# Turning the second token half without GpSimd: g_ffn inside ScalarE's copies, T1 from B11's digits, operands in kept weight rooms

## The chip, the cores and the metric

The kernel runs on one core of a Trainium2 chip. The metric is the device time of one execution in microseconds, and the time given for a kernel is the median of its runs.

## What is computed

One encoder layer for 1024 tokens of width 1024 in fp32. The part that matters here is its end:

```
x  = x + merged @ w_out                  # output projection, residual
h2 = rmsnorm(x, g_ffn)                   # x * rsqrt(mean(x^2) + eps) * g_ffn
x  = x + square(relu(h2 @ w_up)) @ w_down    # 1024 -> 4096 -> 1024
```

Before it stand a first norm, a combined projection, a pooling mixer and a differential attention with eight heads, whose two branches are gated and merged.

## The kernel before

**Digits.** The matrix engine TensorE works on fp32r operands. Each fp32 operand is split into a high digit (a ScalarE copy that rounds, line 125) and a low digit (the difference, line 126, on VectorE or GpSimd). `mm3` (lines 131 to 133) multiplies two such operands in three matmuls: hi x hi, hi x lo, lo x hi.

**Seven products.** Each large product is cut into 2 x 2 blocks and made of seven block products instead of eight (Strassen's scheme in Winograd's form). The right operand of the up projection is h2 transposed, with four blocks: B11 and B21 (the upper and lower 512 features of the first 512 tokens) and B12 and B22 (those of the second 512). From them come T1 = B12 - B11, T2 = B22 - T1, T3 = B22 - B12 and T4 = (B21 - B11) - T3. The left operand is w_up, taken in 16 pairs of 128-column blocks (`up_pair`). The first half of a pair multiplies A11 and A12 with B11 and B21 (banks X and Y, "1" and "2"); its second half makes the sums S1 to S4 of the weight blocks and multiplies them with T2, T1, T3, T4 and B22 ("6", "5", "7", "4", "3"). The first halves of four pairs (AHEAD = 4) need only B11 and B21.

**The output projection's tail.** The string `O_TAIL` writes the order out by hand: "7t" and "4t" are the last products for token tile t (128 tokens) of the second half, "nt" turns tile t of the first half. A product's bank is added to its partial sum by VectorE (L791), and the result is stored to `yd` (L950).

**Norm and turn.** `norm_scale` squares a token tile on ScalarE (L964), forms the mean on VectorE (L965, L256) and its power -1/2 on GpSimd (L257), scales the rows by it on ScalarE (L968) and multiplies by g_ffn, broadcast over the partitions as `gfb`, on VectorE (L971). `norm_turn` transposes eight 128x128 blocks on TensorE (L980) into two PSUM banks `hb`. For the first token half, `first_half` splits the banks into digits of B11 and B21, and stores a copy r11 of the turned B11 and d21 = B21 - r11 to DRAM (`nd`, L993, L994). For the second half, `second_half` loads r11 back into t1 (L1097), has VectorE subtract it from the bank (L1099: T1) and the result from the other bank (L1100: T2), and has ScalarE copy both banks over the tile y (L1102, L1103). `combine` then makes the digits of T1, T3, B22 and T4; the subtractions for T3 and T4 (L1113, L1119) and T3's low digits run on GpSimd.

**Rooms.** Left operands of the up projection (`a_op`) stand in eight rooms of 4 KB per partition: two for A11 (`pw1`), six for all others (`pw`). They lie where the weight rooms of the mixing phase (pool `wpool`, tag W, eight rooms) lay, and a room waits for the last reader of the room below it. Weights of the output projection stand in those W rooms, except sets 6 and 7, which have rooms of their own (tag fw). Scratch tiles come from `ev` (nine rooms), and `finish` takes a new one for each result.

**Order.** The Tile framework orders the instructions of each engine by priorities (`tc.cur_priority`) and resources. Each engine works through its own queue in order. In the code below, `second_scale` for all four tiles and `second_half(4)` have the priorities of the steps "4t"; tiles 5 to 7 follow between the first halves of pairs 0 and 1.

Of the kernel before, what the change touches and what calls it, by code (L numbers as in the profile page):

```python
# [56 lines left out]
O_TAIL = "a0 70 n0 71 n1 72 n2 40 n3 73 41 42 43"  # L57
# [6 lines left out]
def encoder_kernel(  # L64
# [55 lines left out]
    def f(ap):  # L120
        return ap.bitcast(F32)
# [6 lines left out]
    def mm3(ps, lhs_hi, lhs_lo, rhs_hi, rhs_lo, first, last, more=False):  # L128

        kw = {"skip_group_check": True} if more else {}  # L130
        nc.tensor.matmul(ps, lhs_hi, rhs_hi, start=first, stop=False, **kw)  # L131
        nc.tensor.matmul(ps, lhs_hi, rhs_lo, start=False, stop=False, **kw)  # L132
        nc.tensor.matmul(ps, lhs_lo, rhs_hi, start=False, stop=last, **kw)  # L133
# [3 lines left out]
    def wt(shape, name, dt=F32R):  # L137

        wcount[0] += 1
        if wcount[0] > N_QKVW and (wcount[0] - N_QKVW - 1) % (N_W + N_FW) >= N_W:  # L140
            return fw_tile(shape, name, dt)
        return wpool.tile(shape, dt, tag="W", name=name, bufs=N_W)

    def fw_tile(shape, name, dt=F32R):
        return wpool.tile(shape, dt, tag="fw", name=name, bufs=N_FW)
# [255 lines left out]
    with ExitStack() as ph:  # L401
# [75 lines left out]
        nc.sync.dma_start(rows[20:21, :], g_sub)  # L477

# [441 lines left out]
    def w_room(shape, name):  # L920
        return wpool.tile(shape, F32R, tag="W", name=name, bufs=N_W)

# [35 lines left out]
    def norm_scale(t, src, sq):  # L958

        ss = const.tile([P, 2], F32, tag="nss", name=f"nss{t}", bufs=2)  # L960
        rs = const.tile([P, 1], F32, tag="nrs", name=f"nrs{t}", bufs=2)
        yn = y[t]
        for j in range(2):
            nc.scalar.activation(sq, src[j], AF.Square, accum_out=ss[:, j : j + 1])  # L964
        nc.vector.tensor_scalar(rs, ss[:, 0:1], ss[:, 1:2], 1.0 / D, op0=ALU.add, op1=ALU.mult)  # L965
        rsq(rs, rs, 1, 1.0)
        for j in range(2):
            scaled[t] = nc.scalar.activation(yn[:, j * 512 : (j + 1) * 512], src[j], AF.Copy, scale=rs)  # L968
        for j in range(2):
            js = slice(j * 512, (j + 1) * 512)  # L970
            nc.vector.tensor_tensor(yn[:, js], yn[:, js], gfb[:, js], op=ALU.mult)  # L971
# [11 lines left out]
    nd = dram.tile([2, 4, P, 4, P], F32, name="nd")  # L983

    def first_half(t):
# [7 lines left out]
        nc.sync.dma_start(nd[0, t], r11)  # L993
        nc.sync.dma_start(nd[1, t], d21)  # L994
# [6 lines left out]
    prio = {}  # L1001
# [45 lines left out]
    for step in O_TAIL.split():  # L1047
# [7 lines left out]
        elif step[0] == "a":  # L1055
            for d in range(4):
                a_set("4", d)
        elif step[0] == "n":
            first_half(t)
        else:  # L1060
            o_product(Y[t], "4", t, ws["4"])
            k = half(t, 0)
            add(dve, k, Y[t], k)
            y_done(k, 4 + t, 0)
            prio[4 + t] = tc.cur_priority
# [5 lines left out]
    pw1 = pool_of(hs, "pw1", 2)  # L1071
    pw = pool_of(hs, "pw", N_OP - 2)
# [13 lines left out]
    kept_b = {}  # L1086
    T1s, T2_made = {}, {}

    def second_scale(t):
        y[t] = py[t % 4].tile([P, D], F32, tag="y", name=f"y{t}")  # L1090
        norm_scale(t, [half(t - 4, 0), half(t, 0)], y[t][:, 0:512])

    def second_half(t):
# [8 lines left out]
        nc.scalar.copy(kept_b[t][:, 0], b12)  # L1102
        nc.scalar.copy(kept_b[t][:, 1], b22)  # L1103
        T2_made[t] = b_split("T2", c0, t2, dve)

    def combine(q):
        for t in range(4, NT):
# [26 lines left out]

    def u_product(ps, j, a):
        hi, lo = Bq[SIDES[j][1]]
        for k in range(4):
            mm3(
# [4 lines left out]
    def a_op(p, name, src, eng):  # L1143
        a = (pw1 if name == "11" else pw).tile([P, 2, 4, P], F32R, tag="op", name=f"A{name}_{p}")
# [3 lines left out]
    def up_pair(p):  # L1148
# [16 lines left out]
        def finish(q, ps, part):  # L1165
            r = ev(f"u{q}_{p}")
            add(dve, r, ps, part)
# [101 lines left out]
    hs.close()  # L1269
    mlp_ps.close()  # L1270
# [171 lines left out]
```

## Time and profile before

| | us |
|---|---|
| median of 3 runs | 1551.07 (1550.24 to 1551.65) |
| the profiled execution | 1551.25 |
| its span, first to last instruction | 1549.4 |
| granted TensorE clock, mean | 0.999 |

The span is the time from the first to the last instruction in the trace; the time of the execution has some 2 us around it. Engines are named as in the profile: PE is TensorE's matmuls, PEld its weight loads, DVE VectorE, ACT ScalarE, POOL GpSimd, SP the engine whose queue issues most DMAs. A line such as `[1.66 <-ACT y L1102]` says that the engine had been idle for 1.66 us, and that ScalarE's instruction of line 1102 on a tile y ended last of what it waited for. A trailing number in a tile's name is left out.

### The profile page before, as it was taken

What the parts mean: (1) busy time and instruction counts of PE and PEld (TensorE: products, weight loads), DVE (VectorE), ACT (ScalarE), POOL (GpSimd) and SP (SyncE); (2) the same over time, 40 slices, a digit from 0 to 9 for tenths busy, and PEclk for the clock granted to TensorE, in tenths of its full rate; (3) what the DMA queues carried; (4) which work ended last, traced back from release to release, by engine and by line L of the source; (5) the groups of instructions that cost most, each with busy time, mean ns of one, the idle gap of its engine ahead of it and who ended that gap; (6) DMA issues with size and microseconds to landing.
All of it is one profiled execution on the core that took longest, in us unless ns stands there. A gap on an engine that the chain in (4) does not pass through costs nothing. (4 is left out here: it accounts for less than half of the span.)

```text
span 1549.4 us, 21730 instructions
## 1 busy us (share of the span) xinstructions
PE 1524.4 (98%) x7601; PEld 1314.4 (85%) x7601; DVE 1025.6 (66%) x2113; ACT 801.7 (52%) x1642; POOL 411.0 (27%) x481
## 2 busy tenths in 40 slices
PE   7999999999999999999999998999999999999999
PEld 6999999999999999888888886788888788888887
DVE  7777767677777778634644898766665668556572
ACT  5656555556555655534642586555555634333331
POOL 5424242434344443219745514000000000000000
PEclk9999999999999999999999999999999999999999
DMA  7112121111112121249757434554342789537650
GB/s 226 44 53 67 37 66 44 61 51 47 58 40 68 35 88 49 73 150 377 260 170 225 148 143 143 177 177 150 136 137 109 278 314 386 175 123 258 224 190 28
DMA packets 170280, 216.37 MB, mean 140 GB/s; under 512 B 10341, under 2 KB 104250, under 8 KB 170170
## 3 DMA queue, kind: packets, MB, share of 16 engines
q1 hardware_dynamic: 152762, 187.67, 36.8%
q10 hardware_dynamic: 17408, 27.30, 4.7%
q8 instruction: 60, 0.98, 0.3%
q14 instruction: 50, 0.41, 0.1%
HBM read 156.18 MB, written 58.75 MB: 139 GB/s over the span
## 5 line engine op out<-in xcount | busy, mean ns | idle before, releaser
L131 PE MATMUL z<-wqkv,hT 128*128 128x384 f32 x512 | 175.1, 342 | 0.0
L133 PE MATMUL z<-wqkv,hT 128*128 128x384 f32 x512 | 174.2, 341 | 0.5 <-DVE hT L126 0.3
L132 PE MATMUL z<-wqkv,hT 128*128 128x384 f32 x512 | 174.4, 341 | 0.0
L627 ACT ACTIVATE s<-s,nm 128x256 f32<-128x256 f32 (+7 forms) x128 | 99.7, 780 | 74.6 <-DVE nm L619 71.7
L257 POOL TENSOR_TENSOR ms<-ms,mhalf 128x4 f32<-128x4 f32 x64 | 65.2, 1018 | 206.7 <-DVE ms L256 196.4
L131 PE MATMUL g<-hT,fwgate 128*128 128x512 f32 x256 | 101.0, 395 | 0.0
L133 PE MATMUL g<-hT,fwgate 128*128 128x512 f32 x256 | 100.6, 394 | 0.0
L132 PE MATMUL g<-hT,fwgate 128*128 128x512 f32 x256 | 100.5, 393 | 0.0
L131 PEld LDWEIGHTS z<-wqkv,hT 128*128 128x128 f32 x512 | 97.1, 190 | 2.9 <-ACT hT L125 0.6
L133 PEld LDWEIGHTS z<-wqkv,hT 128*128 128x128 f32 x512 | 96.9, 189 | 2.6 <-DVE hT L126 1.4
L132 PEld LDWEIGHTS z<-wqkv,hT 128*128 128x128 f32 x512 | 97.1, 190 | 1.7
L619 DVE CUSTOM_DVE_ANT_0 s<-sc,dist 128x512 f32<-128x512 f32 (+3 forms) x128 | 74.3, 585 | 24.2 <-PE sc L617 23.3
L126 DVE TENSOR_TENSOR AS<-s,AS 128x512 fp32r<-128x512 f32 x64 | 44.9, 705 | 34.4 <-ACT AS L125 34.4
L616 PE MATMUL sc<-K,Q 128*128 128x512 f32 (+2 forms) x192 | 67.3, 356 | 0.4 <-DVE nm L619 0.4
L126 POOL TENSOR_TENSOR wqkv<-rqkv,wqkv 128x384 fp32r<-128x384 f32 x60 | 62.9, 1062 | 14.1 <-ACT wqkv L125 11.7
L617 PE MATMUL sc<-K,Q 128*128 128x512 f32 (+2 forms) x192 | 66.1, 349 | 0.0
L126 POOL TENSOR_TENSOR fwgate<-frgate,fwgate 128x512 fp32r<-128x512 f32 x32 | 43.9, 1374 | 63.2 <-ACT fwgate L125 63.2
L133 PEld LDWEIGHTS g<-hT,fwgate 128*128 128x128 f32 x256 | 48.1, 188 | 9.6
L131 PEld LDWEIGHTS g<-hT,fwgate 128*128 128x128 f32 x256 | 48.1, 188 | 9.1 <-ACT go L375 0.2
L132 PEld LDWEIGHTS g<-hT,fwgate 128*128 128x128 f32 x256 | 48.1, 188 | 8.8
L133 PE MATMUL ba<-yT,wba 128*128 128x512 f32 x128 | 50.4, 395 | 0.0
L132 PE MATMUL ba<-yT,wba 128*128 128x512 f32 x128 | 50.4, 395 | 0.0
(452 smaller groups left out, 4625.9 us busy)
## 6 DMA issues: line engine op xcount, KB each, us to landing
wd<-in_w_down_dram SPq DMA_DIRECT2D x56, 512.0 KB, 5.6
wu<-in_w_up_dram SPq DMA_DIRECT2D x32, 512.0 KB, 5.1
udS<-us SPq DMA_DIRECT2D x64, 256.0 KB, 2.3
ur<-udS SPq DMA_DIRECT2D x32, 512.0 KB, 3.4
rqkv<-in_w_in_dram SPq DMA_DIRECT2D x64, 192.0 KB, 2.9
ud<-u ACTq DMA_DIRECT2D x48, 256.0 KB, 2.1
ur<-ud SPq DMA_DIRECT2D x24, 512.0 KB, 5.0
frgate<-in_w_gate_dram SPq DMA_DIRECT2D x32, 256.0 KB, 2.8
```

The lines of the kernel that those rows point to most:

```text
L126: return (lo_eng or nc.vector).tensor_tensor(lo, src, f(hi), op=ALU.subtract)
L131: nc.tensor.matmul(ps, lhs_hi, rhs_hi, start=first, stop=False, **kw)
L132: nc.tensor.matmul(ps, lhs_hi, rhs_lo, start=False, stop=False, **kw)
L133: nc.tensor.matmul(ps, lhs_lo, rhs_hi, start=False, stop=last, **kw)
L257: nc.gpsimd.tensor_tensor(dst, dst, mhalf[:, :n], op=ALU.pow)
L616: nc.tensor.matmul(dst, Q[:, i, 0, :], rhs, start=True, stop=False)
L617: nc.tensor.matmul(dst, Q[:, i, 1, :], rhs, start=False, stop=True)
L619: nc.vector.tensor_tensor_reduce(out=s[i][:, c : c + w], in0=sc[:, 0:w], in1=dist[:, o0 + c : o0 + c + w], scale=2.0 ** -(h + 1), scalar=B ...
L627: nc.scalar.activation(s[i][:, 0:n], s[i][:, 0:n], AF.Exp, bias=last, scale=-1.0, accum_out=Z[:, i, t : t + 1])
```

## The change

- The scaling and the turning of the second token half move into the tail's written order ("st" and "tt"): tiles 4 and 5 are turned there, into the projection's banks. Tiles 6 and 7 are turned behind product 1 of pair 0 and of pair 1 (`issue_after(made["1"])`).
- For the second half g_ffn is no longer multiplied in by VectorE before the turn. After it, features lie on the partitions, and ScalarE's copies out of the banks, now eight of 128x128 in place of two of 128x512, scale by a column of `cols`, into which g_ffn's rows are loaded at the start.
- For the first half, scaling and g_ffn become one `scalar_tensor_tensor` on VectorE.
- T1 is the kept copy less B11's high digit less its low digit; r11 is no longer stored or loaded.
- The subtractions and low digits for T3 and T4 go from GpSimd to VectorE.
- The weight rooms split into two tags of four, W0 and W1, in a pool that stays open through the up projection. Operands A11 and A12 take W0, all others W1. Of the output projection's sets, 2 and 3 take W0, and 1, 5 and 4 take W1.
- `finish` writes its sum over the partial product's scratch tile.

The power on GpSimd (L257) stays. The diff, cut to its core:

```diff
-O_TAIL = "a0 70 n0 71 n1 72 n2 40 n3 73 41 42 43"
+O_TAIL = "a0 70 n0 71 n1 72 n2 40 s0 n3 73 41 s1 42 t0 s2 43 t1 s3"
...
+    ops = ctx.enter_context(ExitStack())
+    wpool = ops.enter_context(tc.tile_pool(name="wpool", bufs=1))
...
-    wpool = mix.enter_context(tc.tile_pool(name="wpool", bufs=1))
+    fwpool = mix.enter_context(tc.tile_pool(name="fwpool", bufs=N_FW))
...
-        return wpool.tile(shape, dt, tag="W", name=name, bufs=N_W)
+        return w_tile(shape, name, (wcount[0] - 1 - (N_QKVW if wcount[0] > N_QKVW else 0)) % (N_W if wcount[0] <= N_QKVW else N_W + N_FW) // 4 % 2, dt)
+
+    def w_tile(shape, name, i, dt=F32R):
+        return wpool.tile(shape, dt, tag=f"W{int(i)}", name=name, bufs=N_W // 2)
...
+        nc.sync.dma_start(rows[21:29, :], g_ffn[0].rearrange("(r p) -> r p", p=P))
...
-        room = fw_tile if j in "67" else w_room
+        room = fw_tile if j in "67" else lambda shape, name: w_tile(shape, name, j not in "23")
...
         for j in range(2):
-            scaled[t] = nc.scalar.activation(yn[:, j * 512 : (j + 1) * 512], src[j], AF.Copy, scale=rs)
-        for j in range(2):
             js = slice(j * 512, (j + 1) * 512)
-            nc.vector.tensor_tensor(yn[:, js], yn[:, js], gfb[:, js], op=ALU.mult)
+            if t < 4:
+                nc.vector.scalar_tensor_tensor(yn[:, js], src[j], rs, gfb[:, js], op0=ALU.mult, op1=ALU.mult)
+            else:
+                scaled[t] = nc.scalar.activation(yn[:, js], src[j], AF.Copy, scale=rs)
...
-        nc.sync.dma_start(nd[0, t], r11)
-        nc.sync.dma_start(nd[1, t], d21)
+        nc.sync.dma_start(nd[t], d21)
...
+    def second_turn(t, b):
+        kept_b[t] = y[t].rearrange("p (q a b) -> p q a b", q=2, a=4)
+        for j in range(2):
+            for i in range(4):
+                k = 4 * j + i
+                nc.scalar.activation(
+                    kept_b[t][:, j, i, :], b[j][:, i, :], AF.Copy, scale=cols[:, 21 + k : 22 + k]
+                )
...
+        elif step[0] == "s":
+            second_scale(4 + t)
+        elif step[0] == "t":
+            second_turn(4 + t, norm_turn(4 + t, lambda j, name: o_bank(name, 2 * (t % 2) + j)))
...
-    pw1 = pool_of(hs, "pw1", 2)
-    pw = pool_of(hs, "pw", N_OP - 2)
...
+        if after is not None:
+            with tc.issue_after(after.ins):
+                second_turn(t, norm_turn(t, lambda j, name: bm.tile([P, 512], F32, tag="ZW"[j], name=name)))
...
-        nc.sync.dma_start(t1, nd[0, t - 4])
-        b12, b22 = norm_turn(t, lambda j, name: bm.tile([P, 512], F32, tag="ZW"[j], name=name))
-        sub(dve, t1, b12, t1)
-        sub(dve, t2, b22, t1)
-        kept_b[t] = y[t].rearrange("p (q a b) -> p q a b", q=2, a=4)
-        nc.scalar.copy(kept_b[t][:, 0], b12)
-        nc.scalar.copy(kept_b[t][:, 1], b22)
+        cs = slice(c0, c0 + P)
+        sub(dve, t1, kept_b[t][:, 0], f(Bq["11"][0][:, :, cs]))
+        sub(dve, t1, t1, f(Bq["11"][1][:, :, cs]))
+        sub(dve, t2, kept_b[t][:, 1], t1)
...
-                sub(pool, t3, b22, t3)
-                b_split(q, c0, t3, pool)
+                sub(dve, t3, b22, t3)
+                b_split(q, c0, t3, dve)
...
-                nc.sync.dma_start(b22, nd[1, t - 4])
-                sub(pool, b22, b22, t3)
+                nc.sync.dma_start(b22, nd[t - 4])
+                sub(dve, b22, b22, t3)
...
-        a = (pw1 if name == "11" else pw).tile([P, 2, 4, P], F32R, tag="op", name=f"A{name}_{p}")
+        a = w_tile([P, 2, 4, P], f"A{name}_{p}", name not in ("11", "12"))
...
-        def finish(q, ps, part):
-            r = ev(f"u{q}_{p}")
-            add(dve, r, ps, part)
+        def finish(q, ps, r):
+            add(dve, r, ps, r)
...
-    for t in range(4, NT):
-        tc.cur_priority = prio[t]
-        second_scale(t)
-    tc.cur_priority = prio[NT - 1]
     second_half(4)
-    tc.cur_priority = now
-    for p in (0, 0):
-        next(pairs[p])
     second_half(5)
-    second_half(6)
-    next(pairs[1])
-    second_half(7)
+    prio, tc.cur_priority = tc.cur_priority, now
+    for p in range(2):
+        for _ in range(2 - p):
+            next(pairs[p])
+        now, tc.cur_priority = tc.cur_priority, prio
+        second_half(6 + p, made["1"])
+        prio, tc.cur_priority = tc.cur_priority, now
```

More of the change, by code (lines that the diff above doesn't have):

```diff
@@ L132, in mm3 @@
         nc.tensor.matmul(ps, lhs_hi, rhs_lo, start=False, stop=False, **kw)
-        nc.tensor.matmul(ps, lhs_lo, rhs_hi, start=False, stop=last, **kw)
+        return nc.tensor.matmul(ps, lhs_lo, rhs_hi, start=False, stop=last, **kw)
     wcount = [0]
@@ L981, in norm_turn @@
         return [b.rearrange("p (a b) -> p a b", a=4) for b in ps]
-    nd = dram.tile([2, 4, P, 4, P], F32, name="nd")
+    nd = dram.tile([4, P, 4, P], F32, name="nd")
     def first_half(t):
@@ L999, in o_bank, with second_scale @@
         return p.tile([P, 512], F32, tag=tag, name=name)
-    prio = {}
+    kept_b = {}
+    def second_scale(t):
+        y[t] = py[t % 4].tile([P, D], F32, tag="y", name=f"y{t}")
+        norm_scale(t, [half(t - 4, 0), half(t, 0)], y[t][:, 0:512])
+    def second_turn(t, b):
[6 more added lines that the diff above has]
+                )
     ws = {j: w_set(j) for j in "12"}
@@ L1084, in encoder_kernel, with second_half @@
         Bq[q] = tuple(hpT[q].tile([P, 4, 512], F32R, tag="h", name=f"B{q}{i}") for i in "hl")
[L1086 removed]
     T1s, T2_made = {}, {}
[L1089 to L1093, printed above, removed]
+    def second_half(t, after=None):
         c0 = (t - 4) * P
+        if after is not None:
+            with tc.issue_after(after.ins):
+                second_turn(t, norm_turn(t, lambda j, name: bm.tile([P, 512], F32, tag="ZW"[j], name=name)))
         t1, t2 = (ev(f"{n}_{t}", (P, 4, P)) for n in ("t1", "t2"))
         T1s[t] = t1
[L1097 to L1103 removed]
+        cs = slice(c0, c0 + P)
+        sub(dve, t1, kept_b[t][:, 0], f(Bq["11"][0][:, :, cs]))
+        sub(dve, t1, t1, f(Bq["11"][1][:, :, cs]))
+        sub(dve, t2, kept_b[t][:, 1], t1)
         T2_made[t] = b_split("T2", c0, t2, dve)
@@ L1133, in encoder_kernel @@
     ADDS = "673"
+    made = {}
     def u_product(ps, j, a):
@@ L1137, in u_product @@
         for k in range(4):
-            mm3(
+            made[j] = mm3(
                 ps, a[:, 0, k, :], a[:, 1, k, :], hi[:, k, :], lo[:, k, :],
@@ L1269, in encoder_kernel @@
     hs.close()
+    ops.close()
     mlp_ps.close()
```

5 lines of the change are left out of this document (1 added, 4 removed).

## The prediction

> **What bounds the kernel now.** The page is read first, for the engine that fills the span.
>
> ```profile
> span 1549.4 us, 21730 instructions
> PE 1524.4 (98%) x7601; PEld 1314.4 (85%) x7601; DVE 1025.6 (66%) x2113; ACT 801.7 (52%) x1642; POOL 411.0 (27%) x481
> ```
>
> TensorE (PE) works 1524.4 of 1549.4 us. The change takes no matmul away, so all it can gain lies in PE's 25 us of idle time, and of those only where an edited step stands behind the wait. The second view is the busy time by stretches, cut where PE has holes: the end of the output projection, and the passage into the up projection.
>
> ```profile
> 880.00:912.00 32.00, 32.00 (x159) 26.80 (x158) 25.83 (x51) 22.43 (x48) 6.88 (x8) 1.00 0.42 158
> 912.00:970.00 58.00, 50.11 (x220) 38.90 (x219) 52.68 (x76) 41.79 (x81) 20.09 (x14) 0.97 0.40 123
> ```
>
> The columns are PE, weight load, VectorE (DVE), ScalarE (ACT) and GpSimd (POOL). From 880 to 912 PE has no idle time. From 912 to 970 it idles 58.00 - 50.11 = 7.89 us, at a granted clock of 0.97, and DVE, 66% busy over the span, is busy 52.68 of 58 us. The third view, PE's instructions in order of time, lists the holes and who ended them.
>
> ```profile
> 914.34 0.50 PE L131 MATMUL X<-B11h,A 128*128 128x512 f32 x1 [0.45 <-ACT A L125]
> ...
> 937.67 0.66 PE L980 MATMUL hb<-identf,y 128*128 128x128 f32 x4 [1.66 <-ACT y L1102]
> 940.53 0.50 PE L131 MATMUL Y<-B21h,A 128*128 128x512 f32 x1 [2.20 <-DVE u L791]
> 940.87 0.40 PE L132 MATMUL Y<-B21l,A 128*128 128x512 f32 x1
> 941.10 0.39 PE L133 MATMUL Y<-B21h,A 128*128 128x512 f32 x1
> ...
> 942.24 0.63 PE L131 MATMUL Y<-B21h,A 128*128 128x512 f32 x1
> 942.66 0.63 PE L132 MATMUL Y<-B21l,A 128*128 128x512 f32 x1
> ...
> 946.97 0.50 PE L132 MATMUL Z<-BT1l,AS 128*128 128x512 f32 x1 [1.15 <-DVE BT1l L126]
> ...
> 953.53 0.50 PE L131 MATMUL X<-BT3h,AS 128*128 128x512 f32 x1 [1.04 <-ACT U L1190]
> ...
> 962.62 0.50 PE L131 MATMUL Z<-BT1h,AS 128*128 128x512 f32 x1 [0.40 <-DVE u L791]
> ...
> 968.75 0.50 PE L131 MATMUL X<-BT2h,AS 128*128 128x512 f32 x1 [0.62 <-ACT AS L125]
> ...
> 969.85 0.50 PE L133 MATMUL X<-BT2h,AS 128*128 128x512 f32 x1 [0.37 <-DVE AS L126]
> ```
>
> The eight waits sum to 7.89 us, the whole hole. Seven of the eight, all but the first, are VectorE's work or ScalarE's work behind it. After the two long ones the matmuls slow: 940.87 to 941.10 is 0.23 us from start to start, 942.24 to 942.66 is 0.42. About eight steps lie 0.2 us apart too far, so the slow clock costs some 1.6 us more. **The passage is worth 7.89 + 1.6 = 9.5 us**, and VectorE sets it.
>
> The only other hole that an edited step touches is at the end of the up projection.
>
> ```profile
> 1231.54 0.59 ACT L1190 COPY U<-X 128x512 f32<-128x512 f32 x1 [0.67 <-DMA ud<-u]
> ```
>
> ```profile
> 1232.18 0.50 PE L131 MATMUL X<-BT3h,AS 128*128 128x512 f32 x1 [1.83 <-ACT U L1190]
> ```
>
> PE waits 1.83 us for ScalarE's copy of the last pair's U2, and that copy sat 0.67 us until a store of a u tile had landed: the copy's scratch tile was not free.
>
> **The change part by part. GpSimd out of the passage.** DVE and POOL in order of time, where they overlap:
>
> ```profile
> 928.18 0.69 DVE L794 TENSOR_TENSOR s<-wu,wu 128x512 f32<-128x512 f32 x1
> 928.79 0.69 DVE L126 TENSOR_TENSOR BT1l<-t,BT1h 128x512 fp32r<-128x512 f32 x1
> 929.40 1.80 DVE L794 TENSOR_TENSOR s<-wu,s 128x512 f32<-128x512 f32 x1
> ```
>
> ```profile
> 928.90 1.74 POOL L794 TENSOR_TENSOR y<-y 128x512 f32<-128x512 f32 x1 [2.93 <-ACT y L1103]
> 930.61 1.75 POOL L126 TENSOR_TENSOR BT3l<-y,BT3h 128x512 fp32r<-128x512 f32 x1
> ```
>
> VectorE's operations follow each other every 0.60 us until GpSimd starts at 928.90; the next takes 1.80 and ends when GpSimd's ends. The groups of the stretch give the sum of this:
>
> ```profile
> L126 DVE TENSOR_TENSOR A<-wu,A 128x512 fp32r<-128x512 f32 x12 | 8.9, 774 | 0.0
> L126 DVE TENSOR_TENSOR AS<-s,AS 128x512 fp32r<-128x512 f32 x10 | 7.7, 794 | 0.0
> ...
> L126 DVE TENSOR_TENSOR BT2l<-t,BT2h 128x512 fp32r<-128x512 f32 x4 | 5.4, 1345 | 0.1
> L126 DVE TENSOR_TENSOR B22l<-y,B22h 128x512 fp32r<-128x512 f32 x4 | 4.2, 1079 | 0.0
> L971 DVE TENSOR_TENSOR y<-y,gfb 128x512 f32<-128x512 f32 x6 | 3.9, 685 | 0.8 <-ACT y L968 0.8
> L794 DVE TENSOR_TENSOR s<-wu,s 128x512 f32<-128x512 f32 x4 | 3.9, 962 | 0.0
> L126 DVE TENSOR_TENSOR BT4l<-y,BT4h 128x512 fp32r<-128x512 f32 x4 | 3.7, 956 | 0.0
> ```
>
> ```profile
> L794 POOL TENSOR_TENSOR y<-y 128x512 f32<-128x512 f32 x8 | 12.3, 1550 | 17.6 <-DMA y<-nd 11.1 <-ACT y L1103 6.5
> L126 POOL TENSOR_TENSOR BT3l<-y,BT3h 128x512 fp32r<-128x512 f32 x4 | 6.1, 1525 | 3.2 <-ACT BT3h L125 3.2
> ```
>
> An undisturbed one takes 685 ns. Above it: 4 x 0.66 (BT2l), 4 x 0.39 (B22l), 4 x 0.28 (s), 4 x 0.27 (BT4l), 10 x 0.11 (AS), 12 x 0.09 (A): 8.6 us of VectorE's 52.68 are spent beside these 12 GpSimd operations. The 12 move to VectorE at 0.60 each: +7.2. T1 from B11's two digits takes two subtractions in place of one, +4 x 0.60 = 2.4. Six multiplications by g_ffn fall away in the stretch, 6 x 0.60 = -3.6. A11 and A12 of the first two pairs get rooms last read by product 3, long before 912, so their four subtractions can go into VectorE's free time before 912 (32.00 - 25.83 = 6.2 us): -2.4. **Sum: 9.6 - 3.6 - 2.4 - 8.6 = -5.0 us of VectorE's work**. And the tiles come earlier: tokens 4 and 5 are now turned inside the projection's tail, where before the turn of token tile 5 came in the midst of the X and Y products:
>
> ```profile
> 923.83 1.03 PE L980 MATMUL hb<-identf,y 128*128 128x128 f32 x8
> ```
>
> GpSimd's power for the norms stays.
>
> **ScalarE.** A tile's two copies out of PSUM become eight with a scale.
>
> ```profile
> L1102 ACT COPY y<-hb x4: 565/582/586, 918.5 to 942.8; 128x512 f32<-128x512 f32 x4
> ```
>
> ```profile
> L125 ACT CAST V<-z 128x128 fp32r<-128x128 f32 x64 | 16.7, 261 | 0.2 <-DVE s L636 0.2
> ```
>
> At 261 ns for the nearest 128x128 reading of PSUM, a token tile costs 8 x 0.261 - 2 x 0.582 = 0.93 us more, four of them 3.7. ScalarE is busy 41.79 of 58, so 16 us of idle time cover it. Without that cover 0.93 would fall on the path once for the last tile; below nothing only if a scaled copy were shorter than a cast. I take 0.
>
> **First half: scalar_tensor_tensor** in place of a scaled copy and a multiplication, 8 times.
>
> ```profile
> L278 DVE SCALAR_TENSOR_TENSOR hn<-x,rs,gmb x16: 741/747/1778, 8.3 to 42.8; 128x512 f32<-128x512 f32 x16
> ```
>
> 747 against 685 ns: 8 x 0.06 = 0.5 us more on VectorE, in a stretch with 6.2 us free and no idle PE, and ScalarE loses eight passes there. Cost 0; at most 0.5. The Trainium skill, "Vector Engine (DVE) Microarchitecture Reference", section "Points that are easy to get wrong", speaks against it: this operation with two SBUF sources that aren't bf16 runs at half throughput. By that rule the eight would take an estimated 8 x 0.69 = 5.5 us more and fill VectorE before 912; the row, with both sources fp32 in SBUF, shows 747 ns, so the trace does not bear it out.
>
> **DMAs.** Eight transfers of nd (four stores of r11, four loads of t1) go. One 4 KB load of g_ffn rows is added on SP's queue at the start, ahead of later rows of x:
>
> ```profile
> L274 ACT ACTIVATE hn<-x 128x1024 f32<-128x1024 f32 x7 | 7.4, 1062 | 0.2 <-DMA x<-in_x_dram 0.2
> ```
>
> ScalarE waits only 0.2 us for those rows; I take 0, with 0.2 as the upper end.
>
> **Rooms.** Five operands of a pair's second half share four rooms, before six with A12. Four products are 4 x 12 x 0.23 = 11 us, an operand's subtraction and a cast about as long 1.4 us, so I take 0; the bounds are 0 and one late operand in the passage, 1.4. A sum written over x1, z5, U3 and U2 saves four of a pair's twelve scratch tiles; it meets the 0.67 us wait above, between 0 and 1.83.
>
> **Sum.** Hole by hole: 0.45 goes (operands early); 1.66 goes (tokens 6 and 7 are copied out by ScalarE alone, not behind VectorE's subtractions); 2.20 is a bank held for VectorE's add, and half goes, since VectorE is still nearly full until the T digits are made; 1.15 goes (T1 is made before the products need it); the 1.6 of slow clock goes with the long waits; of the last four, 2.43 together, half goes, as T4 and the second pair's sums still queue on VectorE. That is 0.45 + 1.66 + 1.10 + 1.15 + 1.6 + 1.2 = 7.2, and 0.67 at the end: **7.8 us**. The profiled run took 1551.25 (span 1549.4 and 1.85 around it), so 1543.4; the median of the runs is 0.18 lower, so **1543.2 us**.
>
> **The rivals.** *All closes.* VectorE's -5.0 us is more than what is left at 962 to 970, and the whole 1.83 goes with the scratch tile: 9.5 + 1.8 = 11.3, 1539.8 us. Against it: VectorE stays over 80% busy.
>
> *The load takes the wait over.* The second half of pair 1's weights gets its room when T4's digits are done.
>
> ```profile
> 951.09 1.01 SPq L1153 DMA_DIRECT2D wu<-in_w_up_dram  x2
> ```
>
> ```profile
> 955.78 0.69 DVE L791 TENSOR_TENSOR s<-wu 128x512 f32<-128x512 f32 x1 [2.40 <-DMA wu<-in_w_up_dram]
> ```
>
> ```profile
> 959.12 0.39 PE L131 MATMUL X<-BT2h,AS 128*128 128x512 f32 x1
> ```
>
> If T4 is no earlier, pair 1 again starts at 959.12, PE stands idle before it, and the gain is one product of pair 0 done by then, 2.7, and the 1.4 us of later holes: 4.1, so 1547.0. Against it: VectorE has less to do before T4.
>
> *VectorE grows (slower).* In 912 to 970, if its stretched operations are long for another reason than GpSimd, the 8.6 us stay, VectorE has 9.6 - 3.6 = 6.0 us more, PE waits that much longer and saves only 0.45: 1556.6. It decides from a relief under 3.6 us (6.0 less the 2.4 moved). Against it: the 1.80 us row ends with GpSimd's.
>
> *It doesn't do what it says:* the planner keeps the order of waits, each wait is replaced by an equal one, and only 0.45 goes: 1550.6.
>
> **How the numbers follow.** Forecast 0.48 (its own range 1541 to 1546), all closes 0.16, load 0.15, VectorE grows 0.14, nothing 0.07. 0.2% is 3.1 us, about what a measurement of this kernel can tell from no change. The load case lies near that edge; I count 0.10 of it as faster. Faster 0.48 + 0.16 + 0.10 = 0.74, same 0.05 + 0.07 = 0.12, slower 0.14. The range goes from just under "all closes" to just over "nothing", 1539.5 to 1550.8, and leaves out the slower case.
>
> **What would show it.** Right: PE's idle time from 912 to 970 falls from 7.89 to about 2.3 us at a clock of 1.00; BT2l, B22l and BT4l take 0.68 us; the first X product follows the last turn without a wait; no copy of U2 waits for a store. Wrong: VectorE's 128x512 operations still take over 1 us, PE waits at L980 for unscaled rows, or a new wait stands at an operand's room after 1000.

## The result and the profile after

Over ten runs each, the kernel before took 1550.97 us (1550.11 to 1552.24) and the changed one 1547.47 us (1545.17 to 1548.52). The ratio is 0.9974, with a 95% interval of 0.9964 to 0.9984. The change is faster, by 3.5 us by the medians and 4.0 by the ratio. The forecast was 7.8 us less, 1543.2. The profiled execution of the changed kernel took 1546.10 us.

Line numbers of the changed kernel: digits L127 (ScalarE, high) and L128 (VectorE, low), matmuls L133 to L135, adds L797, subtractions L800, squares L967, scales L975 and L973, turns L984, ScalarE's copies of the turned tiles L1015, the power L262. The page of the changed kernel, engines and span:

```profile
span 1544.3 us, 21667 instructions
...
PE 1522.9 (99%) x7601; PEld 1314.6 (85%) x7601; DVE 1018.5 (66%) x2121; ACT 799.1 (52%) x1658; POOL 394.0 (26%) x469
```

PE is idle for 1544.3 - 1522.9 = 21.4 us, before for 25.0. Of the 5.1 us that the span lost, 3.6 are idle time. The busy time by stretches, with columns as before (PE, weight load, VectorE, ScalarE, GpSimd, clock):

```profile
880.00:912.00 32.00, 32.00 (x160) 26.75 (x159) 29.72 (x56) 19.57 (x45) 9.96 (x9) 1.00 0.34 123
912.00:970.00 58.00, 54.05 (x244) 44.12 (x243) 48.73 (x84) 46.49 (x106) 4.81 (x2) 0.97 0.33 105
```

In the passage PE idles 58.00 - 54.05 = 3.95 us where it idled 7.89, at the same clock of 0.97. Windows of 1 us show what that mean is made of: one dip, with a granted clock of 0.50 from 921 to 924 (0.89 and 0.91 in the windows beside it). Before, the same dip lies at 942 to 945. VectorE is 4.0 us less busy, ScalarE 4.7 more. PE's instructions in order of time show where the 3.95 us lie, and two more places:

```profile
867.17 0.47 PE L133 MATMUL oX<-wo,A 128*128 128x512 f32 x1 [1.46 <-ACT A L127]
...
915.09 0.39 PE L135 MATMUL oZ<-wo,A 128*128 128x512 f32 x1
915.32 1.03 PE L984 MATMUL hb<-identf,y 128*128 128x128 f32 x8
920.30 0.50 PE L133 MATMUL Y<-B21h,A 128*128 128x512 f32 x1 [3.94 <-ACT y L1015]
920.64 0.51 PE L134 MATMUL Y<-B21l,A 128*128 128x512 f32 x1
...
921.37 0.63 PE L133 MATMUL Y<-B21h,A 128*128 128x512 f32 x1
921.79 0.63 PE L134 MATMUL Y<-B21l,A 128*128 128x512 f32 x1
...
924.52 0.40 PE L135 MATMUL Y<-B21h,A 128*128 128x512 f32 x1
924.75 0.39 PE L133 MATMUL X<-B11h,A 128*128 128x512 f32 x1
...
1231.15 0.39 PE L135 MATMUL Z<-B22h,AS 128*128 128x512 f32 x1
1231.94 1.19 PE L133 MATMUL Da<-w_0h,u_0h 128*128 128x512 f32 x4 [0.40 <-ACT w_0h L127]
1233.45 0.50 PE L134 MATMUL Da<-w_0l,u_0h 128*128 128x512 f32 x1 [0.32 <-DVE w_0l L128]
```

All eight holes of before are gone from the passage. One new hole of 3.94 us stands in their place, behind the turn of token tile 5, and after it the matmuls are 0.42 apart (921.37 to 921.79) until 924, where 0.23 is normal (924.52 to 924.75). A second new hole, 1.46 us, lies at 867, inside the output projection, of which the prediction read only the end, from 880 on. At the end of the up projection the wait of 1.83 us for U2 has gone; 0.40 and 0.32 us remain, for the first down-projection weights.

By stages: the last matmul of the projection started at 912.62 before and at 915.09 now. That is 2.5 us later: 0.8 for a turn of eight transposes that used to come after it, and the other 1.7 about what the hole at 867 costs. The first matmul of the down projection started at 1237.75 and now at 1231.94. So passage and up projection gave 2.47 + 5.81 = 8.3 us, 7.5 without the turn that only moved. The down projection was 0.7 us longer in this execution. 7.5 - 1.7 - 0.7 = 5.1 us, the difference of the spans.

### The profile page after: what moved, and what is told of

Read it like the earlier page. It is cut to its first block, busy times and chain, and to the rows that moved or that the text cites. A ratio compares the mean times of both kernels' runs of the same rounds, so it can differ in the third digit from the quotient of the medians.

```text
span 1544.3 us, 21667 instructions
## 1 busy us (share of the span) xinstructions
PE 1522.9 (99%) x7601; PEld 1314.6 (85%) x7601; DVE 1018.5 (66%) x2121; ACT 799.1 (52%) x1658; POOL 394.0 (26%) x469
## 4 chain that ended last, share of the span: by engine, by line
PE 93%; DVE 2%; SPq 2%; DMA 1%; ACT 1%; issue 1%; POOL 0%; POOLq 0%; ACTq 0%
PE z L135 6%; PE z L133 6%; PE z L134 6%; PE Da L135 4%; PE Da L134 4%; PE g L135 4%; PE g L134 4%; PE g L133 4%; PE Da L133 4%; PE Db L135 3%; PE Db L134 3%; PE X L133 3%; PE X L134 3%; PE X L135 3%; PE Db L133 3%; PE sc L622 2%
## 5 line engine op out<-in xcount | busy, mean ns | idle before, releaser
L135 PE MATMUL z<-wqkv,hT 128*128 128x384 f32 x512 | 174.0, 340 | 1.2 <-DVE hT L128 1.1
L133 PE MATMUL z<-wqkv,hT 128*128 128x384 f32 x512 | 175.1, 342 | 0.0
L262 POOL TENSOR_TENSOR ms<-ms,mhalf 128x4 f32<-128x4 f32 x64 | 65.9, 1030 | 208.3 <-DVE ms L261 196.8
L133 PE MATMUL g<-hT,fwgate 128*128 128x512 f32 x256 | 101.0, 394 | 0.0
L135 PE MATMUL g<-hT,fwgate 128*128 128x512 f32 x256 | 100.6, 394 | 0.0
L135 PEld LDWEIGHTS z<-wqkv,hT 128*128 128x128 f32 x512 | 96.9, 189 | 3.1 <-DVE hT L128 1.9
L133 PEld LDWEIGHTS z<-wqkv,hT 128*128 128x128 f32 x512 | 97.0, 189 | 2.9 <-ACT hT L127 0.7
L128 POOL TENSOR_TENSOR wqkv<-rqkv,wqkv 128x384 fp32r<-128x384 f32 x60 | 63.4, 1072 | 15.5 <-ACT wqkv L127 15.3
L128 DVE TENSOR_TENSOR AS<-s,AS 128x512 fp32r<-128x512 f32 x64 | 43.3, 687 | 31.4 <-ACT AS L127 31.3
L128 POOL TENSOR_TENSOR fwgate<-frgate,fwgate 128x512 fp32r<-128x512 f32 x32 | 42.9, 1341 | 62.9 <-ACT fwgate L127 62.9
L135 PEld LDWEIGHTS g<-hT,fwgate 128*128 128x128 f32 x256 | 48.1, 188 | 9.5
L133 PEld LDWEIGHTS g<-hT,fwgate 128*128 128x128 f32 x256 | 48.1, 188 | 9.1 <-ACT go L380 0.2
L135 PE MATMUL ba<-yT,wba 128*128 128x512 f32 x128 | 50.4, 395 | 0.0
```

The source lines that it names most:

```text
L128: return (lo_eng or nc.vector).tensor_tensor(lo, src, f(hi), op=ALU.subtract)
L135: return nc.tensor.matmul(ps, lhs_lo, rhs_hi, start=False, stop=last, **kw)
L262: nc.gpsimd.tensor_tensor(dst, dst, mhalf[:, :n], op=ALU.pow)
```

## The new hole, read from ScalarE

Every product needs its PSUM bank, and the bank that the next product (a Y) wants holds tile 5's turned rows until ScalarE has copied them out. ScalarE of the changed kernel in order of time:

```profile
913.24 1.12 ACT L1015 ACTIVATE y<-hb,cols 128x128 f32<-128x128 f32 x4
914.24 0.64 ACT L967 ACTIVATE y<-mp 128x512 f32<-128x512 f32 x1
...
914.86 1.15 ACT L1015 ACTIVATE y<-hb,cols 128x128 f32<-128x128 f32 x4
915.86 0.66 ACT L127 CAST AS<-s 128x512 fp32r<-128x512 f32 x1
916.37 0.68 ACT L967 ACTIVATE y<-mp 128x512 f32<-128x512 f32 x1
...
916.99 1.17 ACT L127 CAST AS<-s 128x512 fp32r<-128x512 f32 x2
918.02 0.66 ACT L127 CAST BT1h<-t 128x512 fp32r<-128x512 f32 x1
918.54 0.66 ACT L127 CAST A<-wu 128x512 fp32r<-128x512 f32 x1
919.06 1.19 ACT L1015 ACTIVATE y<-hb,cols 128x128 f32<-128x128 f32 x4
920.07 0.68 ACT L127 CAST BT2h<-t 128x512 fp32r<-128x512 f32 x1
920.58 1.22 ACT L1015 ACTIVATE y<-hb,cols 128x128 f32<-128x128 f32 x4
```

ScalarE has no gap here. Tile 4's second four copies run until 916.0. Tile 5 is turned by 916.35, but its first four copies start only at 919.06: five casts and a square are ahead of them in ScalarE's queue. They end at 920.25, and PE goes on at 920.30.

VectorE was what the change meant to relieve, and was relieved. Its groups in the passage (columns: count, busy time, mean ns of one):

```profile
L128 DVE TENSOR_TENSOR BT2l<-t,BT2h 128x512 fp32r<-128x512 f32 x4 | 2.7, 681 | 0.0
...
L128 DVE TENSOR_TENSOR B22l<-y,B22h 128x512 fp32r<-128x512 f32 x4 | 2.6, 682 | 0.0
L128 DVE TENSOR_TENSOR BT3l<-y,BT3h 128x512 fp32r<-128x512 f32 x4 | 2.6, 683 | 1.1 <-ACT BT3h L127 1.1
```

BT2l takes 681 ns where it took 1345, B22l 682 where it took 1079. What is left on GpSimd, the power of the norms, has grown instead:

```profile
911.42 0.55 POOL L262 TENSOR_TENSOR nrs<-nrs,mhalf 128x1 f32<-128x1 f32 x1 [2.61 <-DVE nrs L261]
920.70 3.85 POOL L262 TENSOR_TENSOR nrs<-nrs,mhalf 128x1 f32<-128x1 f32 x1 [8.73 <-DVE nrs L261]
```

A 128x1 power takes 0.55 us at 911 and 3.85 us at 920. VectorE beside it:

```profile
920.44 0.68 DVE L128 TENSOR_TENSOR A<-wu,A 128x512 fp32r<-128x512 f32 x1
...
923.45 0.68 DVE L800 TENSOR_TENSOR t<-y,t 128x512 f32<-128x512 f32 x1
```

Six subtractions of two SBUF tiles each follow one another without a gap from 920.44 to 924.13, and the power ends 0.4 us after the last. Beside the short power at 911, VectorE's operation read one operand from a PSUM bank (`d<-hb,r`, 911.35 to 912.04). The Trainium skill, "SBUF — State Buffer", section "Who interferes with whom", has GpSimd share one pair of SBUF ports with VectorE, as an exclusive lock. Both traces agree that one engine holds the other up. Before, VectorE's operation of 1.80 us ended at 931.20, 0.56 us after GpSimd's at 930.64, about as long as one takes by itself (0.60). Here GpSimd's power ends only after VectorE's run of subtractions. That is not so every time: the next power, at 927.20, took 0.97 us in the midst of three such operations (927.07 to 928.96).

## The experiments

All ratios are to the kernel before, run beside them. "From after" means that the edit was made to the changed kernel, "on before" that it was made to the one before. Three things were to be told apart. Is the hole at 920 the price of ScalarE's copies, of the banks, or of the power behind them? Does the gain come from GpSimd's absence, or from the rest of the change, which only happened beside it? And do the rooms and the in-place sum do what the prediction said, the one nothing and the other all of the tail?

### What makes the hole at 920

**Two copies per tile instead of eight**, from after:

```diff
-            for i in range(4):
-                k = 4 * j + i
-                nc.scalar.activation(
-                    kept_b[t][:, j, i, :], b[j][:, i, :], AF.Copy, scale=cols[:, 21 + k : 22 + k]
-                )
+            nc.scalar.copy(kept_b[t][:, j], b[j])
```

> The changed kernel, but each turned tile of the second half is copied out of its banks by two ScalarE copies of 128x512 without a scale, instead of eight of 128x128; g_ffn is left out of the second token half. In the changed kernel PE has one long hole, 3.94 us at 920.30, waiting for ScalarE's copies of token tile 5. Theory A (place in ScalarE's queue: the copies of tile 5 stand behind squares and casts, and tile 5's bank is the bank of pair 1's Y): the shorter copies of tiles 4 and 5 bring the hole down by their 2 x 0.93 us at most, to 2 to 3 us, and the time by 1 to 2 us. Rival B (the eight copies themselves are the cost): the hole falls under 0.5 us and the time by 4 us or more against the changed kernel (to a ratio of 0.995 or less).

1543.28 us, ratio 0.9948 (0.9934 to 0.9961). PE's line at the hole, and the passage:

```profile
918.00 0.50 PE L133 MATMUL Y<-B21h,A 128*128 128x512 f32 x1 [2.07 <-ACT y L1013]
```

```profile
912.00:970.00 58.00, 55.13 (x252) 44.69 (x251) 50.05 (x87) 42.73 (x84) 5.89 (x2) 1.00 0.39 117
```

The hole falls from 3.94 to 2.07 us and the clock stays at 1.00: about half of the hole goes with the eight short copies; the other half is still a wait for tile 5's copies, which stand behind the same casts and square. The time falls by more than the hole does, 4.0 us against the change by the ratios, and so by more than the theory's 1 to 2. The slow matmuls behind the hole are gone too (some 3.4 us at half clock, so about 1.7 us), and the hole at 867 was 0.56 us shorter in this trace (0.90).

**Other banks for the turns inside the projection**, from after, so that no product waits for tile 5's copies:

```diff
-            second_turn(4 + t, norm_turn(4 + t, lambda j, name: o_bank(name, 2 * (t % 2) + j)))
+            second_turn(4 + t, norm_turn(4 + t, lambda j, name: o_bank(name, j)))
```

> The changed kernel, but tile 5 is turned into the same two banks as tile 4 (those of the projection's z tag), so that no bank of an early X or Y product holds a turned tile. Theory A: the 3.94 us hole and its 1.5 to 2 us of slow clock go; PE's idle time from 912 to 970 is under 1.5 us, and the time falls by 4 to 6 us against the changed kernel, ratio to before 0.994 to 0.995. Rival C (the next thing is as late: the last product's add on VectorE, at 917.25, frees the bank of pair 0's X): a hole of about 2 us stays ahead of X, and the time falls by 2 us, ratio about 0.996. Rival D (the copies of tile 4 hold up the turn of tile 5, and PE with it): the hole is 3 us or more again, at L984.

1546.33 us, 0.9965 (0.9952 to 0.9977). PE idles 3.94 us in the passage, as much as in the change, in other places:

```profile
939.65 0.50 PE L133 MATMUL Y<-B21h,A 128*128 128x512 f32 x1 [1.36 <-DVE x L797]
944.38 0.49 PE L133 MATMUL Z<-BT1h,AS 128*128 128x512 f32 x1 [1.66 <-ACT BT1h L127]
945.79 0.80 PE L134 MATMUL Z<-BT1l,AS 128*128 128x512 f32 x1 [0.92 <-DVE BT1l L128]
```

None of the theories had this, though the time is the one that rival C gave. The hole at 920 went, so the bank was its place, but PE runs into the T1 digits instead, whose chain (tile 7's norm, turn, copies, subtractions, digits) is not earlier. The wait at the bank hid a second limit of nearly the same length.

**No power on GpSimd in the second half**, from after:

```diff
-        rsq(rs, rs, 1, 1.0)
+        if t < 4:
+            rsq(rs, rs, 1, 1.0)
+        else:
+            nc.vector.tensor_scalar(rs, rs, 1.0, EPS, op0=ALU.mult, op1=ALU.add)
+            nc.vector.reciprocal(rs, rs)
```

> The changed kernel, but for the second token half the norm's power on GpSimd is replaced by a reciprocal on VectorE, so that GpSimd does nothing there; the square root is left out, the rows come out scaled wrongly. In the changed kernel GpSimd's power for tile 6 takes 3.85 us (others 0.55) while VectorE works beside it, and tile 6 is scaled at 924.6. Theory K (this power sets when the T1 digits of tiles 6 and 7 are ready, about 945, but PE loses its time earlier, at 920.30, to ScalarE's queue): tile 6 is scaled 3 us earlier, the hole at 920 stays within 0.7 us of 3.94, and the time is within 1.5 us of the changed kernel (ratio to before 0.9965 to 0.998). Rival L (power and hole are one chain): the hole shrinks by 2 us or more.

1545.41 us, 0.9959 (0.9945 to 0.9972). The square root is left out here. The hole at 920 stays, at 3.37 us. The power is not its cause. Without it the time is some 2 us shorter by the medians and the ratios, more than theory K's 1.5, though the intervals overlap; 0.7 us of it lies at 867, where the hole is 0.73 in this trace.

**Both edits together:**

> Both: tile 5 turned in tile 4's banks, and the reciprocal on VectorE in place of GpSimd's power (the square root left out). With the banks alone the hole at 920 went, but three holes at 939.65, 944.38 and 945.79 came, 3.94 us in sum, behind VectorE's add and the T1 digits. Theory K: T1's digits are 3 us earlier, PE's idle time from 912 to 970 falls from 3.94 to under 1.5 us at a clock of 1.00, and the time to 0.993 to 0.995 of before. Rival M (the T1 digits wait for VectorE's full queue, not for the norm): idle time stays above 3 us and the ratio at 0.996 to 0.997.

1544.16 us, 0.9950 (0.9936 to 0.9963). PE idles 58 - 55.59 = 2.41 us, 0.94 and 0.83 of it for the T1 digits, at a clock of 1.00. The T1 chain is 3 us earlier without the power (its first product starts at 941.26, not 944.38), so the power does sit in that chain. The holes were not as small as the stronger theory wanted.

### GpSimd, put back and taken out alone

**GpSimd back**, from after:

```diff
-                sub(dve, t3, b22, t3)
-                b_split(q, c0, t3, dve)
+                sub(pool, t3, b22, t3)
+                b_split(q, c0, t3, pool)
...
-                sub(dve, b22, b22, t3)
+                sub(pool, b22, b22, t3)
```

> The changed kernel, but the subtractions for T3 and T4 and T3's low digits run on GpSimd again, as before. Theory G (what GpSimd does to VectorE's operations made the passage VectorE's): operations of VectorE of 1.1 to 1.8 us come back beside GpSimd's, holes behind VectorE of 2 to 5 us in total come back after 930, and the kernel is 2 to 5 us slower than the changed one, ratio to before about 1.000. Rival H (the earlier turns and the earlier operands alone made the passage short): VectorE's operations are stretched again, but PE's idle time changes by less than 1 us and so does the time.

1552.81 us, 1.0004 (0.9995 to 1.0013): the whole gain is gone. Its passage, PE's two holes there and one group of VectorE:

```profile
912.00:970.00 58.00, 50.60 (x217) 40.69 (x216) 51.22 (x69) 43.65 (x101) 20.29 (x15) 0.91 0.32 97
```

```profile
920.46 0.50 PE L133 MATMUL Y<-B21h,A 128*128 128x512 f32 x1 [3.82 <-ACT y L1015]
950.40 0.80 PE L134 MATMUL Z<-BT1l,AS 128*128 128x512 f32 x1 [3.58 <-DVE BT1l L128]
```

```profile
L128 DVE TENSOR_TENSOR B22l<-y,B22h 128x512 fp32r<-128x512 f32 x4 | 6.1, 1551 | 2.2 <-ACT B22h L127 2.2
```

The stretched operations are back, and with them a wait of 3.58 us for T1's low digits, behind a bank wait that is the change's own.

**Only GpSimd's part of the change**, on before: the same three operations moved from `pool` to `dve`, nothing else.

> The kernel before, with only this part of the change: the subtractions for T3 and T4 and T3's low digits run on VectorE instead of GpSimd. By the prediction's terms VectorE gets 7.2 us of work and loses 8.6 us of stretching, net -1.4 us. Theory G: no operation of 128x512 on VectorE is over 0.8 us in the passage, and the time falls by 1 to 3 us (ratio 0.998 to 0.9995). Rival H (the move alone brings nothing; it needs the earlier turns): ratio 0.9995 to 1.001, and the holes behind VectorE's adds and BT1l stay within 1 us of 7.89 in sum.

1545.47 us, 0.9960 (0.9945 to 0.9976): 6.2 us less, where the theory said 1 to 3. By the ratios that is more than the whole change brought (0.9974), but the intervals overlap. Passage, the group that was most stretched, and the end of the up projection:

```profile
912.00:970.00 58.00, 54.39 (x246) 42.83 (x246) 55.47 (x96) 44.74 (x87) 1.39 (x2) 1.00 0.44 135
```

```profile
L126 DVE TENSOR_TENSOR BT2l<-t,BT2h 128x512 fp32r<-128x512 f32 x4 | 2.7, 680 | 0.0
```

```profile
1225.78 0.50 PE L131 MATMUL X<-BT3h,AS 128*128 128x512 f32 x1 [1.71 <-ACT U L1190]
```

VectorE is busy 55.47 of 58 us, 6.7 more than in the change, and PE still loses less: 3.61 us in five holes, the longest 0.91, at a clock of 1.00. In the same 58 us VectorE also got through more, 96 instructions (76 before, 84 in the change), so its busy time is not that of the same work. The reading that fits is that PE waits for when single operations of VectorE end, and not for VectorE's total; no run tests that by itself. The tail's wait for U2 stays.

### Rooms and scratch tiles

**The sum over its own scratch tile**, on before with GpSimd out:

```diff
-        def finish(q, ps, part):
-            r = ev(f"u{q}_{p}")
-            add(dve, r, ps, part)
+        def finish(q, ps, r):
+            add(dve, r, ps, r)
```

> The kernel before with two parts of the change: GpSimd's subtractions and digits for T3 and T4 on VectorE, and the sums of finish written over the partial product's scratch tile. Theory P (the 1.7 us hole before the last X product comes from the scratch tiles): the hole falls under 0.5 us, and the time by 1 to 2 us against VectorE alone, to a ratio of 0.9945 to 0.9955. Rival Q (in the changed kernel it went because the down projection's digits stand in rooms that come free earlier): the hole stays above 1.2 us and the ratio at 0.996.

1546.05 us, 0.9964 (0.9951 to 0.9978), no gain, and the tail keeps its hole (2.05 us). The prediction's reason for the tail was wrong.

**The kept rooms**, on the same kernel: the two tags W0 and W1, the pool kept open, and A11 and A12 in W0, as in the change.

> The kernel before with two parts of the change: GpSimd's subtractions and digits for T3 and T4 on VectorE, and the rooms as the change has them (tags W0 and W1, kept past the projection). Theory R (the rooms do two things, whatever else is changed: set 1 in W1 makes the hole at 867, and the down projection's digits over rooms that come free earlier shorten the hole before the last pair's X or the first Da product): a hole of 0.9 to 1.7 us at about 867, which VectorE's part alone does not have; at 1215 to 1245 the wait for U2 goes and at most 0.8 us is left of 1.71; ratio to before within 0.001 of VectorE's part alone (0.996). Rival S (either of the two comes from the planner or from the earlier turns): no hole at 867, or 1.5 us and more left at the end.

1543.80 us, 0.9953 (0.994 to 0.9967):

```profile
866.43 0.47 PE L133 MATMUL oX<-wo,A 128*128 128x512 f32 x1 [1.23 <-ACT A L127]
...
1229.61 1.19 PE L133 MATMUL Da<-w_0h,u_0h 128*128 128x512 f32 x4 [0.55 <-ACT w_0h L127]
1230.97 0.51 PE L134 MATMUL Da<-w_0l,u_0h 128*128 128x512 f32 x1 [0.17 <-DVE w_0l L128]
```

Of the change's other parts the rooms by themselves bring both things: the hole at 867 appears, and the wait for U2 at the tail is gone.

**The tags exchanged**, from after:

```diff
-        room = fw_tile if j in "67" else lambda shape, name: w_tile(shape, name, j not in "23")
+        room = fw_tile if j in "67" else lambda shape, name: w_tile(shape, name, j in "23")
...
-        a = w_tile([P, 2, 4, P], f"A{name}_{p}", name not in ("11", "12"))
+        a = w_tile([P, 2, 4, P], f"A{name}_{p}", name in ("11", "12"))
```

> The changed kernel with the two room tags exchanged: sets 1, 5 and 4 and the operands other than A11 and A12 take W0, sets 2 and 3 and A11, A12 take W1. In the changed kernel, and in its three variants, PE has a hole of 0.9 to 1.7 us at 867 in the output projection that the kernels without the room split do not have; the loads there come some 4 us later. Theory N (set 1 must wait for the rooms of W1, which the mixing phase frees last, so the loads behind it on SP's queue come late): the hole at 867 falls under 0.4 us, gfb is loaded at 829 to 830 instead of 832.9, and the time falls by 1 to 2 us. Rival O (it is the planner's order, not the rooms): a hole of about 1.5 us stays.

1544.20 us, 0.9949 (0.9935 to 0.9963), and no hole at 867. The trace shows why. The rows of sets 1 and 2 come first, and their digits need weight rooms: ScalarE's first cast of w_out rows starts at 791.75 before, at 807.89 in the change, and at 790.35 with the tags exchanged. Later loads, and all behind them in SyncE's queue, wait for that (the third load of w_out rows: 797.99, 812.78, 795.31). The load of g_ffn, which comes after sets 1 and 2 and three loads of w_sum rows, in before, after, and with the tags exchanged:

```profile
829.01 0.35 SPq L916 DMA_DIRECT2D gfb<-in_g_ffn_dram  x1
```

```profile
832.89 0.79 SPq L922 DMA_DIRECT2D gfb<-in_g_ffn_dram  x1
```

```profile
825.98 0.42 SPq L922 DMA_DIRECT2D gfb<-in_g_ffn_dram  x1
```

In the change the queue is 3.9 us later than before, and 6.9 us later than with the tags exchanged. ScalarE's first cast of the next w_out rows was at 854.28 before; in the change it waits until 858.18. The next rows of w_sum are asked for at 861.91, before at 858.07; their cast waits until 866.04, and the cast of A that PE wants at 867 stands right behind it:

```profile
858.18 0.62 ACT L127 CAST wo<-ro 128x512 fp32r<-128x512 f32 x1 [4.73 <-DMA ro<-in_w_out_dram]
...
866.04 0.62 ACT L127 CAST wo<-ro 128x512 fp32r<-128x512 f32 x1 [1.71 <-DMA ro<-w_sum]
```

**GpSimd out and exchanged rooms**, on before, and without anything else of the change:

> The same with the two tags exchanged (sets 1, 5, 4 and the operands but A11 and A12 in W0). Theory R: no hole at 867 over 0.4 us, at most 0.8 us at the end, the passage as with VectorE's part alone (about 3.6 us in small holes, clock 1.00); 1 to 2.5 us faster than that, ratio 0.994 to 0.9955. Rival S: as before, 0.996.

1543.97 us, 0.9947 (0.9935 to 0.996). No hole at 867, 0.51 and 0.20 us before the down projection, and in the passage 58 - 55.88 = 2.12 us:

```profile
912.00:970.00 58.00, 55.88 (x256) 44.73 (x255) 54.20 (x92) 43.48 (x83) 1.51 (x2) 1.00 0.45 138
```

Two parts of the change, one of them mended, do better than all of it: the interval lies just below that of the change, 0.9964 to 0.9984.

### Everything mended

**Exchanged rooms and other banks**, from after:

> The changed kernel with the tags exchanged and tile 5 turned in tile 4's banks. If the two edits add up: the hole at 867 goes (worth 0.0025 alone) and the holes of 912 to 970 are those of the bank edit, 3 to 4 us in sum behind the T1 digits (worth 0.001 alone): ratio 0.993 to 0.9955. If they don't, because the earlier projection only lengthens the wait for the T1 digits: holes of 4 to 5.5 us and a ratio of 0.995 to 0.997.

1544.16 us, 0.9954 (0.9942 to 0.9967), 3.96 us of holes in the passage, the same three waits as with other banks alone (1.38, 1.66, 0.92). The two edits are no better than the exchange by itself.

**The same with the root by three Heron steps on VectorE**, so that GpSimd has nothing in the second half:

```diff
+            nc.vector.tensor_scalar(rs, rs, 1.0, EPS, op0=ALU.mult, op1=ALU.add)
+            nc.vector.tensor_scalar(h, rs, 0.5, None, op0=ALU.mult)
+            nc.vector.tensor_scalar(u, rs, 0.5, 0.5, op0=ALU.mult, op1=ALU.add)
+            for i in range(3):
...
+                nc.vector.reciprocal(v, u)
+                nc.vector.tensor_tensor(v, v, h, op=ALU.mult)
+                nc.vector.scalar_tensor_tensor(u, u, 0.5, v, op0=ALU.mult, op1=ALU.add)
+            nc.vector.reciprocal(rs, u)
```

> The same, and for the second token half the inverse square root is made on VectorE from three Heron steps on 128x1 (twelve operations a tile, some 2 us more of VectorE's time, in place of GpSimd's power of 0.55 to 4.45 us); nothing is left out. Theory K: holes in 912 to 970 under 2.5 us at a clock of 1.00, ratio 0.9925 to 0.9945, the fastest of all. Rival T (the twelve operations stand in VectorE's queue as long as the power did): holes of 3 to 5 us, ratio as without it.

1541.66 us, 0.9937 (0.9924 to 0.9951), the shortest of all. But its passage is worse, not better: 4.90 us idle at a clock of 0.94, with one wait of

```profile
943.81 0.80 PE L133 MATMUL Z<-BT1h,AS 128*128 128x512 f32 x1 [3.83 <-ACT BT1h L127]
```

The dozen small steps of a tile queue one by one among VectorE's 0.68 us operations: those of tile 7 run from 920.92 to 931.1, 10 us for 14 operations of 0.14 to 0.21. The rival was right on the holes. The short time comes from elsewhere. One stretch of the down projection, of this kernel and of the changed one:

```profile
1300.00:1400.00 100.00, 100.00 (x443) 82.78 (x442) 57.26 (x53) 36.61 (x37) 0.00 (x0) 1.00 0.52 179
```

```profile
1300.00:1400.00 100.00, 100.00 (x439) 82.05 (x438) 57.46 (x54) 36.49 (x37) 0.00 (x0) 1.00 0.53 180
```

443 of PE's matmuls fall in it where the changed kernel has 439, with no idle time and a granted clock of 1.00 in both; 1000 to 1100, 1100 to 1200 and 1400 to 1500 show 443 against 439, 439 and 438. Over the 570 us from 970 on that 1% is an estimated 5 us. From start to start it is 0.2267 us here and 0.2289 in the changed kernel and the one before (1310 to 1390). In the output projection, about 860, it is 0.2267 in the kernel before too. So this kernel keeps a spacing that the others lose behind the passage; all other runs have 438 or 439. The cause stays open. The root by Heron steps is therefore not shown to be worth anything, and the interval overlaps that of the kernel with GpSimd out and the tags exchanged.

## Why the prediction was right and where it was wrong

**GpSimd was the main term: right, and too small.** The stretched operations are gone (BT2l, B22l and BT4l take 681, 682 and 676 ns), and putting GpSimd back alone returns the time of before. Of VectorE's work the sum gave -5.0 us for the whole change; measured, VectorE's busy time fell by 4.0. But taking GpSimd out alone gained 6.2 us while VectorE's busy time rose by 2.8, with 20 more instructions done in the stretch. "VectorE grows" fell: the relief was real. One reading was off, without harm: the row of 1.80 us did not end with GpSimd's but 0.56 us after it.

**The value of the passage: too small.** The forecast counted 7.89 us idle and 1.6 of slow clock. A hole also costs what the idle column doesn't list: at the down projection two matmuls start at 1231.15 and 1231.94, 0.79 apart where 0.23 is normal, though only 0.40 is listed, so 0.16 more; and the first matmul after a hole takes 0.34 to the next start (1233.45 to 1233.79), 0.11 more. That is 0.27 per hole, and 2.2 for the eight: an estimate, from one reading of each part. The 1.6 of slow clock had the right size, but it was not gained: the same dip of the clock now follows the new hole.

**Half of the bank's wait and of the last four: wrong in detail.** All eight went, more than forecast, the last four too. Part of that is luck: PE came 3.94 us later, so what it had waited for was ready. With that hole taken away (other banks), waits for a bank and for T1's digits of 1.36, 1.66 and 0.92 us are back.

**"ScalarE. I take 0": the step that failed.** The price of the copies was right: scaled copies start 0.25 apart (913.24 to 914.24 for four), forecast 0.261. The cover was not there. The text set 16 us of idle time over the whole stretch against the copies. Where tile 5 is turned, from 913 to 921, ScalarE has no idle time at all, and the turn has moved to a place where PE's very next product needs the same bank. The cost was 3.94 us and the slow matmuls behind it, not 0 to 0.93. The forecast put the first X product right behind the last turn without a wait; in the profile the next product, a Y, waits exactly there. Of the passage's two signs for being right, 2.3 us of idle time and a clock of 1.00, neither came (3.95, 0.97).

**"Rooms. I take 0": the second step that failed.** It looked for a late operand in the up projection; PE never waits for one there now. The rooms also serve the output projection's weights, and the split makes the first sets wait for theirs: 1.46 us at 867, in a part of the kernel that the prediction did not read. With its 0.27 the hole is 1.7 us of the profile. Exchanging the tags took 3.3 us off the changed kernel by the medians. Off the kernel before with GpSimd out and the rooms kept it took only 0.0006 of the ratio, inside the intervals. So more than the 1.7 us is not shown.

**The tail: right that it goes, wrong why.** The scratch tile saved nothing; the kept rooms removed the wait. In the forecast it was worth 0.67 of 1.83; all 1.83 went and 0.72 took its place, in waits for the down projection's first digits.

**GpSimd's power stays: true and not costed.** It went from 0.55 to 3.85 us beside VectorE's now denser work.

**scalar_tensor_tensor: right.** The eight take 743 ns on average, forecast 747, and two in a row 1.40 us. PE does not idle there.

```profile
896.04 1.40 DVE L973 SCALAR_TENSOR_TENSOR y<-y,nrs,gfb 128x512 f32<-128x512 f32 x2
```

**"The load takes the wait over": it did not.** VectorE waits 2.97 us for pair 1's weights now, before 2.40, and PE has no wait behind it.

So the time lay inside the range in part by luck, by errors that partly cancel: the relief and the passage were worth more than forecast, and two edits entered at nothing took some 3.5 us (ScalarE's copies, by the two-copies run without its shorter hole at 867) and 1.7 us (rooms) of it back. 1547.47 lies outside the forecast's own range of 1541 to 1546, next to the 1547.0 of the load's rival, whose wait did not come.

## What to carry to other kernels

Idle time that is to cover an edit must be read at the place and time of the edit, in the engine's order of instructions, not as the free share of a stretch: ScalarE was 80% busy over 58 us and 100% busy over the 8 that counted. When a step is moved, ask which bank or room the next instruction of the bound engine wants, and when a pool is split, list every load that shares it, also those of the stage before. A wait that is removed may hide another of the same length, so try each part alone: here one part of the change came out at 0.9960 by itself, and all of it at 0.9974.

## What the runs showed of the hardware that was not expected

- A 128x1 power on GpSimd took 0.55 us beside a VectorE subtraction with one operand in PSUM, and 3.85 us beside six unbroken ones of two SBUF tiles; beside three of those another took 0.97.
- In kernels with one long idle time in the passage, of 3.94, 3.37 and 3.83 us, its granted clock was 0.97, 0.97 and 0.94. With one of 2.07 us, and with several under 1 us each, it was 1.00. With three of 1.36, 1.66 and 0.92 within 7 us it was 0.97. Each dip stands in 1 us windows as 0.50, for some 3.4 us in the changed kernel and from 943 to 949 in the one at 0.94.
- Two kernels at a granted clock of 1.00 and without idle time had 443 and 439 matmuls of the same shape in 100 us, from the up projection on; from 500 to 600 us both had 584. What differs was not found. The faster one has three more small tiles in its constants, which may shift the others' places; that was not tried.
